# Sixteen fullest experts: stationary gate and up weights, tokens moving as one block

## The chip, the cores and the metric

The kernel runs on one core of a Trainium2 chip. The metric is the device time of one execution in microseconds (us). Five engines work side by side: TensorE (PE in the profile, with PEld for its weight loads), VectorE (DVE), ScalarE (ACT), GpSimd (POOL) and SyncE (SP), which here issues most DMA transfers. [...]

## The reference

One decoder layer on 2048 tokens of width 1024, in f32. After a mixer of a state space branch and a windowed attention branch comes the part that matters here, a hierarchical mixture of experts: each token picks one of 4 groups and in it the best 2 of 8 experts, so there are 4096 (token, expert) pairs over 32 experts. Then follow a gated embedding and a final norm. The expert is

```python
def expert_block(args):
    xb, e = args
    return (jax.nn.silu(xb @ w_eg[e]) * (xb @ w_eu[e])) @ w_ed[e]
```

with w_eg and w_eu of 1024 x 512 and w_ed of 512 x 1024. A token's two expert rows are weighted and added.

## The kernel before

**Precision.** Every large product is made of operands split in two parts, hi and lo, in a four-byte type for fast matmuls (fp32r). The product is hi*hi + hi*lo + lo*hi; the helper `mm3` (line 64) issues these three matmuls, which share nothing but their accumulator. A weight unit is 128 x 2048 (1 MB): SP fetches it to a raw buffer (`moe_raw`), ACT casts it to its hi part and DVE subtracts to get the lo part (`moe_split`, lines 1469 and 1470). There are four raw buffers and six pairs of hi and lo buffers, used in turn.

**Blocks of tokens.** The experts are ranked by their number of tokens (`route_tables`). Each rank has a slot of 128 rows; the 16 fullest have a second slot (slots 32 to 47): 128 rows for ranks 0 to 3 (`R1`), 64 rows for ranks 4 to 15 (`R2`). What exceeds these goes to `overflow`, a loop over blocks of 128 rows behind a branch on their number. `moe_in` gathers a slot's token rows from DRAM with an indirect DMA on POOL's queue and turns them on TensorE (line 1359: 8 transposes into PSUM, which ACT and DVE split into hi and lo).

**One expert.** `moe_gu` keeps the tokens stationary and moves the weights: for each of 8 slices k of the width, one matmul of 512 columns for each part of gate and of up. A slot of 128 rows takes 6 matmuls for each k. A slot of 64 rows is packed: its hi and lo tokens stand side by side as one stationary operand of 128 columns, 4 matmuls do for each k, and afterwards ACT copies one half of the result and DVE adds it to the other (lines 1390 to 1393). The result has the tokens on the partitions, so after silu and product `moe_act` turns it on TensorE (line 1409: 4 transposes for a slot) and splits it again. `moe_down` moves the two down units over it, 24 matmuls of 512 columns for 128 rows, 16 for a packed slot, evacuates the sums on ACT and DVE and scatters the rows with an indirect DMA.

**Order.** The experts run in pairs, a full one and an emptier one (ranks 0, 31, 1, 30, ...). In each step the next expert's tokens are fetched, then come this expert's gate and up, the expert before's down, and this one's activations:

```python
acts = self.moe_gu(xs, wt, nm)
if prev is not None:
    self.moe_down(*prev())
hl = self.moe_act(acts, nm)
```

The order inside each engine's queue is made from this program by a scheduler in the framework, which also sets the waits from the use of the buffers; each engine works its queue in order. Accumulators for gate, up and down share six PSUM banks (tag `acc`), the transposes two (tag `tp`). Turned tokens have three buffers for each part, activations three. After the experts, `proj_last` does the remaining part of an embedding projection, in the same buffers.

Of the kernel before, what the change touches and what calls it, by code (L numbers as in the profile page):

```python
# [11 lines left out]
F32 = mybir.dt.float32  # L12
# [11 lines left out]
NE = 32  # L24
NS1 = 48
R2 = 16
R1 = 4
NPA = 5
# [10 lines left out]
NUNIT = _n  # L39


class Kern:
# [1022 lines left out]
    def proj_last(self, n, m):  # L1065
# [137 lines left out]
    def route_tables(self, ctx):  # L1203
# [140 lines left out]
    def moe_in(self, idx, nm, rows=128):  # L1344
# [5 lines left out]
        xh = p.tile([128, 8, 128], F32R, tag="xh", name=f"xh{nm}", bufs=3)  # L1350
        if rows == 64:
            hi, lo = xh[:, :, 0:64], xh[:, :, 64:128]
        else:
            hi, lo = xh, p.tile([128, 8, 128], F32R, tag="xl", name=f"xl{nm}", bufs=3)
# [7 lines left out]
        return (xh, None) if rows == 64 else (hi, lo)  # L1362

    def moe_gu(self, xs, wt, nm):
# [3 lines left out]
        gu = [[ps.tile([128, 512], F32, tag="acc", name=f"{q}{n}", bufs=6) for q in "gu"] for n in nm]  # L1368
        for k in range(8):
            if k % 2 == 0:  # L1370
                wh, wl = wt[k // 2] if isinstance(wt, list) else wt(k // 2)
            s, e = k == 0, k == 7
            for (xh, xl), (g, u) in zip(xs, gu):
                cg = slice((k % 2) * 512, (k % 2) * 512 + 512)
                cu = slice(1024 + (k % 2) * 512, 1024 + (k % 2) * 512 + 512)
                pk = xl is None
                mm(g, xh[:, k], wh[:, cg], start=s, stop=False)  # L1377
                mm(g, xh[:, k], wl[:, cg], start=False, stop=pk and e)  # L1378
                mm(u, xh[:, k], wh[:, cu], start=s, stop=False)  # L1379
                mm(u, xh[:, k], wl[:, cu], start=False, stop=pk and e)  # L1380
                if not pk:
                    mm(g, xl[:, k], wh[:, cg], start=False, stop=e)  # L1382
                    mm(u, xl[:, k], wh[:, cu], start=False, stop=e)  # L1383
        res = []
        for n, (xh, xl), (g, u) in zip(nm, xs, gu):
            a = p.tile([128, 512], F32, tag="act", name=f"a{n}", bufs=3)
            if xl is None:
                a = a[0:64]
                b = p.tile([64, 2, 512], F32, tag="half", name=f"b{n}", bufs=1)
                nc.scalar.copy(b[:, 0], g[64:128])  # L1390
                nc.scalar.copy(b[:, 1], u[64:128])
                V.tensor_tensor(out=a, in0=g[0:64], in1=b[:, 0], op=ALU.add)
                V.tensor_tensor(out=b[:, 1], in0=u[0:64], in1=b[:, 1], op=ALU.add)
                nc.scalar.activation(a, a, AF.Silu)
                V.tensor_tensor(out=a, in0=a, in1=b[:, 1], op=ALU.mult)
            else:
                nc.scalar.activation(a, g, AF.Silu)
                V.tensor_tensor(out=a, in0=a, in1=u, op=ALU.mult)
            res.append(a)
        return res  # L1400

    def moe_act(self, acts, nm):
        nc, p, ps = self.nc, self.mp, self.mps
        hl = []
        for a, n in zip(acts, nm):
            rows = a.shape[0]
            tp = ps.tile([128, 4, 128], F32, tag="tp", name=f"ta{n}")[:, :, 0:rows]
            for k in range(4):
                nc.tensor.transpose(tp[:, k], a[:, k * 128:k * 128 + 128], self.ident[0:rows, 0:rows])  # L1409
            ah = p.tile([128, 4, 128], F32R, tag="ah", name=f"ah{n}", bufs=3)  # L1410
            if rows == 64:
                hi, lo = ah[:, :, 0:64], ah[:, :, 64:128]
            else:
                hi, lo = ah, p.tile([128, 4, 128], F32R, tag="al", name=f"al{n}", bufs=3)
            self.turned = [nc.scalar.copy(hi, tp).ins,  # L1415
                           nc.vector.tensor_tensor(out=lo, in0=tp, in1=hi, op=ALU.subtract).ins]
            hl.append((ah, None) if rows == 64 else (hi, lo))
        return hl

    def moe_down(self, hl, wt, dst, nm):  # L1420
# [3 lines left out]
        for j in range(2):  # L1424
            wh, wl = wt[j] if isinstance(wt, list) else wt(4 + j)
            js = slice(j * 512, j * 512 + 512)
            for (ah, al), yo, d, n in zip(hl, ys, dst, nm):
                y = ps.tile([128, 512], F32, tag="acc", name=f"y{n}{j}", bufs=6)
                rows = 64 if al is None else 128
                for k in range(4):  # L1430
                    c = slice(k * 512, k * 512 + 512)
                    if al is None:
                        mm(y, ah[:, k], wh[:, c], start=k == 0, stop=False)  # L1433
# [322 lines left out]
```

## Time and profile before

| | |
|---|---|
| timed runs | median 2347.01 us of 3 (2344.53 to 2348.16) |
| profiled execution | 2350.74 us, its span 2349.0 us |
| PE busy | 2261.8 us, 96%, 13948 matmuls |
| PEld busy | 1992.6 us |
| DVE busy | 1644.1 us, 70% |
| ACT busy | 1195.1 us, 51% |
| POOL busy | 364.1 us |
| DMA | 515.56 MB, mean 219 GB/s |

The expert stage runs from about 1300 to 2120 us of the span. The profile's matmul durations contain a pipeline's tail and overlap; what a matmul costs in a full queue is the distance from its start to the next start, which is read from the timeline. Records are labelled f32 in the rows for both four-byte types; a plain f32 matmul leaves two records, the fast type one.

### The profile page before, as it was taken

The numbers are of one execution on the slowest core, as the hardware profiler recorded it, in microseconds if no ns is written. First come the engines' busy times: TensorE is split into PE (matmuls) and PEld (weight loads), VectorE is DVE, ScalarE is ACT, GpSimd is POOL, SyncE is SP. The second block draws the span as 40 slices with busy tenths as digits, with TensorE's granted clock in tenths as the row PEclk, the third lists the DMA queues.
The fourth block names the chain that finished last, engine by engine and source line by source line (L and its number), as shares of the span: only waits on it lengthen the run. The fifth ranks groups of instructions, "written<-read, shape, count | busy, mean of one in ns | idle before, by whom it ended". The sixth has DMA issues, their size and how long they took to land. (4 is left out here: it accounts for less than half of the span.)

```text
span 2349.0 us, 36510 instructions
## 1 busy us (share of the span) xinstructions
PE 2261.8 (96%) x13948; PEld 1992.6 (85%) x13948; DVE 1644.1 (70%) x2666; ACT 1195.1 (51%) x1835; POOL 364.1 (16%) x282
## 2 busy tenths in 40 slices
PE   8889998899999999999999799999999999999997
PEld 8789996899999999998887588888887888877876
DVE  8777647788885334445667576677787777776998
ACT  7333335567664323222233565566666666664444
POOL 0043110221120000000001121121221112131122
PEclk9889999899999999999999799999999999999999
DMA  8385453643436546545444788888888888876552
GB/s 319 121 278 169 150 161 107 227 153 122 153 104 207 166 148 220 184 129 178 153 161 161 289 299 305 294 313 305 297 322 326 313 304 300 328 280 236 181 208 106
DMA packets 136082, 515.56 MB, mean 219 GB/s; under 512 B 16416, under 2 KB 34768, under 8 KB 108512
## 3 DMA queue, kind: packets, MB, share of 16 engines
q1 hardware_dynamic: 112544, 429.56, 53.2%
q0 software_dynamic: 23216, 83.37, 9.7%
q8 instruction: 111, 1.82, 0.3%
q14 instruction: 67, 0.55, 0.1%
q10 hardware_dynamic: 144, 0.26, 0.0%
HBM read 407.09 MB, written 102.77 MB: 217 GB/s over the span
## 5 line engine op out<-in xcount | busy, mean ns | idle before, releaser
L1470 DVE TENSOR_TENSOR e_l<-e_r,e_h 128x2048 fp32r<-128x2048 f32 x192 | 438.2, 2290 | 168.9 <-ACT e_h L1469 168.6
L1469 ACT CAST e_h<-e_r 128x2048 fp32r<-128x2048 f32 x192 | 366.3, 1911 | 156.8 <-PE us L1379 49.3
L1377 PE MATMUL gs<-e_h,xhs 128*128 128x512 f32 x384 | 153.1, 399 | 5.7 <-PEq L1530 5.7
L1379 PE MATMUL us<-e_h,xhs 128*128 128x512 f32 x384 | 153.6, 400 | 0.0
L1378 PE MATMUL gs<-e_l,xhs 128*128 128x512 f32 x384 | 150.6, 392 | 0.0
L1380 PE MATMUL us<-e_l,xhs 128*128 128x512 f32 x384 | 150.4, 392 | 0.0
L1445 POOL DMA_INDIRECT yb_d<-yos,rt x48 | 91.4, 1904 | 357.8 <-DVE yos L1441 129.6
L66 PE MATMUL ys<-e_h,ahs 128*128 128x512 f32 x288 | 114.2, 396 | 2.9 <-ACT ahs L1415 2.9
L67 PE MATMUL ys<-e_l,ahs 128*128 128x512 f32 x288 | 116.1, 403 | 0.0
L1348 POOL DMA_INDIRECT xgs<-h_d,rt x48 | 68.1, 1420 | 303.3 <-PE txs L1359 177.5
L68 PE MATMUL ys<-e_h,als 128*128 128x512 f32 x288 | 114.4, 398 | 0.0
L1383 PE MATMUL us<-e_h,xls 128*128 128x512 f32 x288 | 114.2, 397 | 0.0
L1382 PE MATMUL gs<-e_h,xls 128*128 128x512 f32 x288 | 113.3, 394 | 0.0
L68 PE MATMUL pz<-pg_h,pl 128*128 128x512 f32 (+1 forms) x264 | 103.2, 393 | 3.1 <-DVE pl L1591 2.8
L825 POOL TENSOR_TENSOR s<-s,dn 128x1024 f32<-128x1024 f32 (+1 forms) x32 | 63.2, 1975 | 276.9 <-DVE dn L824 159.9
L66 PE MATMUL pz<-pg_h,ph 128*128 128x512 f32 (+1 forms) x264 | 102.4, 389 | 0.0
L67 PE MATMUL pz<-pg_l,ph 128*128 128x512 f32 (+1 forms) x264 | 101.8, 386 | 0.0
L66 PE MATMUL u<-xh,u_h 128*128 128x256 f32 x256 | 72.4, 290 | 17.6 <-DVE ut L458 9.8
L1377 PEld LDWEIGHTS gs<-e_h,xhs 128*128 128x128 f32 x384 | 72.6, 189 | 19.5 <-issue 6.1
L1379 PEld LDWEIGHTS us<-e_h,xhs 128*128 128x128 f32 x384 | 72.4, 189 | 15.0
L1378 PEld LDWEIGHTS gs<-e_l,xhs 128*128 128x128 f32 x384 | 72.6, 189 | 14.5
L1380 PEld LDWEIGHTS us<-e_l,xhs 128*128 128x128 f32 x384 | 72.5, 189 | 14.1
(1484 smaller groups left out, 7337.2 us busy)
## 6 DMA issues: line engine op xcount, KB each, us to landing
e_r<-in_We SPq DMA_DIRECT2D x192, 1024.0 KB, 5.9
m_d<-mo SPq DMA_DIRECT2D x64, 256.0 KB, 3.4
yg<-yb_d SPq DMA_DIRECT2D x15, 1024.0 KB, 7.4
xt<-in_xT SPq DMA_DIRECT2D x16, 512.0 KB, 7.9
sq<-in_x SPq DMA_DIRECT2D x16, 512.0 KB, 5.3
m<-m_d SPq DMA_DIRECT2D x16, 512.0 KB, 5.2
xr<-in_x SPq DMA_DIRECT2D x16, 512.0 KB, 4.6
x_d<-xr POOLq DMA_DIRECT2D x16, 512.0 KB, 3.0
```

The costliest lines, as they stand in the source:

```text
L66: mm(out, ah, bh, start=start, stop=False)
L67: mm(out, ah, bl, start=False, stop=False)
L68: return mm(out, al, bh, start=False, stop=stop)
L1377: mm(g, xh[:, k], wh[:, cg], start=s, stop=False)
L1378: mm(g, xh[:, k], wl[:, cg], start=False, stop=pk and e)
L1379: mm(u, xh[:, k], wh[:, cu], start=s, stop=False)
L1380: mm(u, xh[:, k], wl[:, cu], start=False, stop=pk and e)
L1382: mm(g, xl[:, k], wh[:, cg], start=False, stop=e)
L1383: mm(u, xl[:, k], wh[:, cu], start=False, stop=e)
L1445: nc.gpsimd.indirect_dma_start(out=self.yb_d[:], out_offset=bass.IndirectOffsetOnAxis(ap=d[0:rows], axis=0), in_=yo[0:rows], in_offset=None)
L1469: nc.scalar.copy(hi, raw)
L1470: nc.vector.tensor_tensor(out=lo, in0=raw, in1=hi, op=ALU.subtract)
```

## The change

For the 16 experts with a second slot (`moe_gu_wide`) gate and up weights become the stationary operand, in pieces of 128 x 128, and both slots' tokens move as one block of n = 224, 192 or 160 rows (ranks 0 to 3, 4 to 7, 8 to 15): `more(r)` gives the second slot's 96, 64 or 32 rows. The hi and lo parts of the block lie side by side in one tile (`xw`), so one matmul with 2n columns does w_hi times both, and one with n columns does w_lo times hi. Hi and lo sums stand in two halves of a bank; ACT copies one half and DVE adds it to the other. The results have the hidden index on the partitions and go to `moe_down` without a transpose, after a cast and two subtracts. `moe_gu` for single slots now does 256 gate and 256 up columns at a time over all k, then the other half, since the weight units are cut anew: a unit holds 4 slices k of 256 gate and 256 up columns. Limits of the routing follow (`R3`, `cap`). Turned tokens have one buffer for each part, the block one, activations two.

```diff
 R2 = 16
+R3 = 8
 R1 = 4
+RM = 224
+def more(r):
+    return 32 * ((r < R1) + (r < R3) + (r < R2))
...
# proj_last
-            pr, hi, lo = f("xg", F32, "pr"), p.tile([128, 2, w], F32R, tag="xh", name=f"prh{g[0]}", bufs=3), \
-                p.tile([128, 2, w], F32R, tag="xl", name=f"prl{g[0]}", bufs=3)
+            pr, (t, b) = f("xg", F32, "pr"), ("x", 1) if w > 256 else ("a", 2)
+            hi, lo = (p.tile([128, 2, w], F32R, tag=t + q, name=f"pr{q}{g[0]}", bufs=b) for q in "hl")
...
# route_tables
         stt(cap, rank, R1 - 0.5, r2, ALU.is_lt, ALU.add)
+        stt(cap, rank, R3 - 0.5, cap, ALU.is_lt, ALU.add)
         ts(rk, rank, 128.0, None, ALU.mult)
-        ts(cap, cap, 64.0, 128.0, ALU.mult, ALU.add)
+        ts(cap, cap, 32.0, 128.0, ALU.mult, ALU.add)
...
+    def moe_gu(self, x, wt, nm):
+        nc, p, ps = self.nc, self.mp, self.mps
+        xh, xl = x
+        a = p.tile([128, 512], F32, tag="act", name=f"a{nm}", bufs=3)
+        for j in range(2):
+            gu = ps.tile([128, 512], F32, tag="acc", name=f"gu{nm}{j}", bufs=6)
+            for k in range(8):
+                if k % 4 == 0:
+                    wh, wl = wt[2 * j + k // 4] if isinstance(wt, list) else wt(2 * j + k // 4)
+                c = slice(k % 4 * 512, k % 4 * 512 + 512)
+                self.mm3(gu, xh[:, k], xl[:, k], wh[:, c], wl[:, c], k == 0, k == 7)
+            h = a[:, j * 256:j * 256 + 256]
+            nc.scalar.activation(h, gu[:, 0:256], AF.Silu)
+            nc.vector.tensor_tensor(out=h, in0=h, in1=gu[:, 256:512], op=ALU.mult)
+        return a
+
+    def moe_gu_wide(self, x, n, wt, nm):
+        nc, p, ps = self.nc, self.mp, self.mps
         V, mm = nc.vector, nc.tensor.matmul
+        m = n - 128
+        ahl = p.tile([128, 4, 2 * RM], F32R, tag="aw", name=f"aw{nm}", bufs=1)
+        for j in range(2):
+            acc = [ps.tile([128, 512], F32, tag="acc", name=f"w{nm}{j}{b}", bufs=6)[:, 0:2 * n] for b in range(4)]
+            for kh in range(2):
+                wh, wl = wt[2 * j + kh]
+                for b in (0, 2, 1, 3):
+                    for k in range(4):
+                        c = k * 512 + b * 128
+                        xk = x[:, 4 * kh + k]
+                        s, e = kh == k == 0, kh == 1 and k == 3
+                        mm(acc[b].rearrange("p (a n) -> p a n", a=2), wh[:, c:c + 128], xk, start=s, stop=False)
+                        mm(acc[b][:, 0:n], wl[:, c:c + 128], xk[:, 0], start=False, stop=e)
+            for b in range(2):
+                t = p.tile([128, 512], F32, tag="act", name=f"t{nm}{j}{b}", bufs=3)
+                g, u = t[:, 0:n], t[:, 256:256 + n]
+                aj = ahl[:, 2 * j + b]
+                for q, v in ((b, g), (2 + b, u)):
+                    nc.scalar.copy(v, acc[q][:, n:2 * n])
+                    V.tensor_tensor(out=v, in0=acc[q][:, 0:n], in1=v, op=ALU.add)
+                nc.scalar.activation(g, g, AF.Silu)
+                V.tensor_tensor(out=g, in0=g, in1=u, op=ALU.mult)
+                nc.scalar.copy(aj[:, 0:n], g)
+                V.tensor_tensor(out=aj[:, n + m:2 * n], in0=g[:, 0:128], in1=aj[:, 0:128], op=ALU.subtract)
+                V.tensor_tensor(out=aj[:, n:n + m], in0=g[:, 128:n], in1=aj[:, 128:n], op=ALU.subtract)
+        return [(ahl[:, :, 0:128], ahl[:, :, n + m:2 * n], 128),
+                (ahl[:, :, 128:n + m], None, m) if m <= 64 else (ahl[:, :, 128:n], ahl[:, :, n:n + m], m)]
...
# moe, fetch
+            x = self.mp.tile([128, 8, 2, RM], F32R, tag="xw", name=f"xw{slots[0]}", bufs=1)[:, :, :, 0:128 + m]
+            for q, (s, w) in enumerate(zip(slots, (128, m))):
+                self.moe_in(ix[q], f"s{s}", w, x, 128 * q)
...
# moe, the loop
+            wide = rows > 128
+            acts = self.moe_gu_wide(x, rows, wt, nm[0]) if wide else self.moe_gu(x, wt, nm[0])
             if prev is not None:
                 self.moe_down(*prev())
-            hl = self.moe_act(acts, nm)
+            hl = acts if wide else self.moe_act(acts, nm[0])
...
# pack, on the host: the new weight units
-        return w.reshape(NE, 4, 2, 128, 512).transpose(0, 1, 3, 2, 4)
-    gu = np.stack([rows(g["w_e_gate"][0]), rows(g["w_e_up"][0])], 3).reshape(NE, 4, 128, 2048)
+        return w.reshape(NE, 2, 4, 128, 2, 256).transpose(0, 4, 1, 3, 2, 5)
+    gu = np.stack([rows(g["w_e_gate"][0]), rows(g["w_e_up"][0])], 5).reshape(NE, 4, 128, 2048)
```

`moe_down` takes each block's rows with it: blocks of 64 rows and fewer are packed as before, others (now also 96 rows) take three matmuls for each k.

## Rows read from the trace of the kernel before

**Rows 1.** the page, busy time of an engine, share of the span, instructions.
```profile
PE 2261.8 (96%) x13948; PEld 1992.6 (85%) x13948; DVE 1644.1 (70%) x2666; ACT 1195.1 (51%) x1835; POOL 364.1 (16%) x282
```

**Rows 2.** who waits for whom, PE, 1250 to 2130 us (total us, times, longest).
```profile
PE txs L1359 <- DMA xgs<-h_d,rt: 7.6, 1, 7.6
PE gs L1377 <- PEq L1530: 5.7, 1, 5.7
PE txs L1359 <- DVE xls L1361: 3.0, 1, 3.0
PE ys L66 <- ACT ahs L1415: 2.9, 1, 2.9
```

**Rows 3.** windows: length, then busy us of each engine, PE's granted clock, DMA share, GB/s.
```profile
1500.00:1600.00 100.00, 100.00 (x472) 81.33 (x471) 75.26 (x58) 63.89 (x61) 19.74 (x12) 1.00 0.84 310
1800.00:1900.00 100.00, 100.00 (x471) 80.37 (x470) 77.96 (x63) 65.89 (x62) 17.54 (x13) 1.00 0.87 311
```

**Rows 4.** timeline, gate and up: start us, duration us, engine, line, operation.
```profile
1399.82 0.39 PE L1378 MATMUL gs<-e_l,xhs 128*128 128x512 f32 x1
1401.41 0.39 PE L1379 MATMUL us<-e_h,xhs 128*128 128x512 f32 x1
```

**Rows 5.** timeline, down.
```profile
1411.47 0.40 PE L66 MATMUL ys<-e_h,ahs 128*128 128x512 f32 x1
1414.28 0.40 PE L66 MATMUL ys<-e_h,ahs 128*128 128x512 f32 x1
```

**Rows 6.** timeline, matmuls of 256 columns in the gates' stage.
```profile
899.82 0.28 PE L67 MATMUL gz<-gh1070l,gB_h 128*128 128x256 f32 x1
903.94 0.28 PE L66 MATMUL gz<-gh1071h,gB_h 128*128 128x256 f32 x1
```

**Rows 7.** timeline, transposes (eight merged in one row).
```profile
1406.17 1.04 PE L1359 MATMUL txs<-ident,xgs 128*128 128x128 f32 x8
1522.04 0.71 PE L1359 MATMUL txs<-ident,xgs 64*128 64x64 f32 x8
```

**Rows 8.** groups by line and form, PE, 1300 to 2130 us (busy us, mean ns).
```profile
L1377 PE MATMUL gs<-e_h,xhs 128*128 128x512 f32 x384 | 153.1, 399 | 5.7 <-PEq L1530 5.7
L1409 PE MATMUL tas<-ident,as 128*128 128x128 f32 x144 | 21.1, 272 | 0.0
L1409 PE MATMUL tas<-ident,as 64*128 64x64 f32 x48 | 5.5, 235 | 0.0
```

**Rows 9.** the same of PEld, the whole span.
```profile
L967 PEld LDWEIGHTS lg<-h2l,wrhl 128*36 128x36 f32 x56 | 6.2, 112 | 1.0 <-DVE h2l L961 0.7
L968 PEld LDWEIGHTS lg<-h2h,wrhl 128*72 128x72 f32 x64 | 9.1, 142 | 1.5 <-ACT h2h L960 0.6
L1377 PEld LDWEIGHTS gs<-e_h,xhs 128*128 128x128 f32 x384 | 72.6, 189 | 19.5 <-issue 6.1
L1359 PEld LDWEIGHTS txs<-ident,xgs 64*128 64x128 f32 x96 | 7.6, 138 | 8.4 <-DVE xhs L1361 4.0 <-issue 3.7 <-DVE xls L1361 0.7
```

**Rows 10.** timeline, plain f32 of 128 columns (two records in a row).
```profile
339.98 0.39 PE L568 MATMUL op<-uT,t 128*128 128x128 f32 x2
341.10 0.39 PE L571 MATMUL op<-S,ca 128*128 128x128 f32 x2
```

**Rows 11.** groups by line and form, DVE and ACT, 1300 to 2130 us.
```profile
L1470 DVE TENSOR_TENSOR e_l<-e_r,e_h 128x2048 fp32r<-128x2048 f32 x191 | 436.0, 2290 | 168.9 <-ACT e_h L1469 168.6
L1361 DVE TENSOR_TENSOR xls<-txs,xhs 128x512 fp32r<-128x512 f32 x72 | 48.6, 684 | 13.6 <-ACT xhs L1360 9.2 <-DMA pp_d<-po 4.3
L1361 DVE TENSOR_TENSOR xhs<-txs,xhs 128x256 fp32r<-128x256 f32 x24 | 9.8, 412 | 0.0
L1469 ACT CAST e_h<-e_r 128x2048 fp32r<-128x2048 f32 x190 | 362.7, 1911 | 156.8 <-PE us L1379 49.3 <-PE us L1383 42.3 <-PE ys L1433 36.2
L1360 ACT CAST xhs<-txs 128x512 fp32r<-128x512 f32 x72 | 41.5, 585 | 30.4 <-PE txs L1359 30.4
L1360 ACT CAST xhs<-txs 128x256 fp32r<-128x256 f32 x24 | 8.8, 371 | 0.3
```

More of the change, by code (lines that the diff above doesn't have):

```diff
@@ L1341, in row_index, with moe_in @@
         return done
-    def moe_in(self, idx, nm, rows=128):
+    def moe_in(self, idx, nm, rows=128, into=None, at=0):
         nc, p, ps = self.nc, self.mp, self.mps
@@ L1349, in moe_in @@
                                      in_offset=bass.IndirectOffsetOnAxis(ap=idx[0:rows], axis=0))
-        xh = p.tile([128, 8, 128], F32R, tag="xh", name=f"xh{nm}", bufs=3)
-        if rows == 64:
-            hi, lo = xh[:, :, 0:64], xh[:, :, 64:128]
+        if into is None:
+            hi, lo = (p.tile([128, 8, 128], F32R, tag=f"x{q}", name=f"x{q}{nm}", bufs=1) for q in "hl")
         else:
-            hi, lo = xh, p.tile([128, 8, 128], F32R, tag="xl", name=f"xl{nm}", bufs=3)
+            hi, lo = into[:, :, 0, at:at + rows], into[:, :, 1, at:at + rows]
         for h in range(2):
@@ L1366, in moe_gu @@
+    def moe_gu_wide(self, x, n, wt, nm):
         nc, p, ps = self.nc, self.mp, self.mps
         V, mm = nc.vector, nc.tensor.matmul
[L1368 to L1399, printed above, removed]
@@ L1400, in moe_gu @@
-        return res
-    def moe_act(self, acts, nm):
-        nc, p, ps = self.nc, self.mp, self.mps
[L1404 to L1418, printed above, removed]
+        m = n - 128
@@ new lines, in moe_gu_wide, with moe_act @@
+        return [(ahl[:, :, 0:128], ahl[:, :, n + m:2 * n], 128),
+                (ahl[:, :, 128:n + m], None, m) if m <= 64 else (ahl[:, :, 128:n], ahl[:, :, n:n + m], m)]
+    def moe_act(self, a, nm):
+        nc, p, ps = self.nc, self.mp, self.mps
+        tp = ps.tile([128, 4, 128], F32, tag="tp", name=f"ta{nm}")
+        for k in range(4):
+            nc.tensor.transpose(tp[:, k], a[:, k * 128:k * 128 + 128], self.ident)
+        hi, lo = (p.tile([128, 4, 128], F32R, tag=f"a{q}", name=f"a{q}{nm}", bufs=2) for q in "hl")
+        self.turned = [nc.scalar.copy(hi, tp).ins,
+                       nc.vector.tensor_tensor(out=lo, in0=tp, in1=hi, op=ALU.subtract).ins]
+        return [(hi, lo, 128)]
@@ L1426, in moe_down @@
             js = slice(j * 512, j * 512 + 512)
-            for (ah, al), yo, d, n in zip(hl, ys, dst, nm):
+            for (ah, al, rows), yo, d, n in zip(hl, ys, dst, nm):
                 y = ps.tile([128, 512], F32, tag="acc", name=f"y{n}{j}", bufs=6)
-                rows = 64 if al is None else 128
                 for k in range(4):
@@ L1432, in moe_down @@
                     if al is None:
[L1433 to L1434 removed]
+                        mm(y[0:2 * rows], ah[:, k], wh[:, c], start=k == 0, stop=False)
+                        mm(y[0:2 * rows], ah[:, k], wl[:, c], start=False, stop=k == 3)
                     else:
[L1436 removed]
+                        last = self.mm3(y[0:rows], ah[:, k], al[:, k], wh[:, c], wl[:, c], k == 0, k == 3)
                 if al is None:
[L1438 to L1439 removed]
+                    nc.scalar.copy(yo[0:rows, js], y[rows:2 * rows])
+                    nc.vector.tensor_tensor(out=yo[0:rows, js], in0=y[0:rows], in1=yo[0:rows, js], op=ALU.add)
                 elif j:
[L1441 removed]
+                    self.downed = nc.vector.tensor_copy(yo[0:rows, js], y[0:rows]).ins
                 else:
[L1443 removed]
+                    nc.scalar.copy(yo[0:rows, js], y[0:rows])
                 if j:
@@ L1492, in fetch @@
         def fetch(slots):
-            return [self.moe_in(self.IDX[:, s:s + 1], f"s{s}", 64 if s >= 32 + R1 else 128) for s in slots]
+            ix = [self.IDX[:, s:s + 1] for s in slots]
+            if len(slots) == 1:
+                return self.moe_in(ix[0], f"s{slots[0]}"), 128
+            m = more(slots[0])
+            x = self.mp.tile([128, 8, 2, RM], F32R, tag="xw", name=f"xw{slots[0]}", bufs=1)[:, :, :, 0:128 + m]
+            for q, (s, w) in enumerate(zip(slots, (128, m))):
+                self.moe_in(ix[q], f"s{s}", w, x, 128 * q)
+            return x, 128 + m
         self.wslots((), range(3))
```

13 lines of the change are left out of this document (3 added, 10 removed).

## The prediction

> **What bounds the kernel now.** I read the page first: the matrix engine (PE) is busy for 96% of the span [rows 1]. Then the waits of PE over the whole expert stage: 7.6 us for the first gathered tokens, 5.7 us at the overflow branch, 3.0 us at the second turn, 2.9 us before the last down projection, one of each, and nothing else of weight [rows 2]. Between these PE waits for nothing, and the windows say the same: from 1500 us on PE is busy throughout at a granted clock of 1.00, with VectorE (DVE) at 75 to 78%, ACT at 64 to 66% and the DMA engines at 84 to 87% [rows 3]. So the expert stage is a sum of PE's starts; every nanosecond taken from a matmul's spacing comes off the end, as long as nobody else becomes late. Ends of matmuls overlap, so I count from start to start.
>
> The spacings are: a gate/up matmul with 512 moving columns, seven starts in 1.59 us, 0.227 us each [rows 4]; a down matmul, twelve in 2.81 us, 0.234 us [rows 5]; a matmul with 256 moving columns, 35 in 4.12 us, 0.118 us [rows 6]. Eight transposes of 128 columns last 1.04 us with a tail of about 0.27, so 0.110 us each; of 64 columns, (0.71 - 0.235) / 7 = 0.068 us ([rows 7], the tails from [rows 8]).
>
> **Gate and up of the sixteen wide experts.** L1377 ran 384 times, 8 for each of 48 slots [rows 8]; a slot of 128 rows takes 6 matmuls for each of 8 k (20 such slots are in wide experts), each of the 12 packed ones 4. So an expert with two full slots costs 96 x 0.227 = 21.8 us (4 of them), one with a packed second slot 80 x 0.227 = 18.2 us (12). Afterwards each expert has 64 pairs (2 x 2 x 4 x 4): one matmul with 2n moving columns, one with n, for n = 224 (4 experts), 192 (4), 160 (8). The wide one lies between the measured 256 and 512 columns; on their line (0.109 us over 256 columns) it takes 0.145, 0.173, 0.200 us for n = 160, 192, 224.
>
> The narrow one has no row: no matmul in this operand type moves under 256 columns. Its bounds:
> - Below, the same line carried on: 0.077, 0.091, 0.104 us. That needs weights that load faster than that.
> - In the middle, the weight load. The loads' durations grow evenly: 36 columns 112 ns, 72 columns 142 ns, 128 columns 189 ns [rows 9], so 0.83 ns a column, and 128 columns occupy 107 ns behind a fixed latency of about 82 ns. (A transpose's load lasts only 138 ns, 56 ns over the same latency, and those do come every 68 ns.) A matmul whose own columns need less than 107 ns would then come every 0.118 us, as at 256 columns, where load and columns are equally long.
> - Above, the plain f32 matmul: 128 columns are two records of 0.112 us each (ten starts in 1.12 us) [rows 10], so 0.28, 0.34, 0.39 us.
>
> I take the middle, 0.118 us, since it rests on the loads of just this type. An expert then costs 64 x (0.145 + 0.118) = 16.9 us, 18.6 us, 20.3 us, and the sixteen change by 8 x (16.9 - 18.2) + 4 x (18.6 - 18.2) + 4 x (20.3 - 21.8), unrounded **-14.6 us**. Below it would be -46 us, above +194 us. The moving columns fall by 18%, but half of the new matmuls don't get their share of it: with 192 rows the expert even gets slower.
>
> [...]
>
> **Transposes.** A wide expert's activations come out with the hidden index on the partitions, so its 4 transposes per slot go: of the 144 of 128 columns and the 48 of 64 [rows 8], 80 and all 48, 80 x 0.110 + 48 x 0.068 = **-12.1 us**. Gathered tokens are still turned; 32 turns of 128 columns become 96 columns (by the line between 0.068 and 0.110, -0.02 us each), 64 of 64 become 32 (between 0 and half, I take none): **-0.7 us** (to -2.9).
>
> **Down.** The second block of 96 rows keeps three matmuls for each k, those of 64 and 32 rows the packed two; all still move 512 columns and their number stays 1056: 0. The narrow experts keep 48 gate/up matmuls, now half after half; if these take the down spacing, 768 x 0.007 = +5 us; I take 0, as the pattern of operands is the old one.
>
> **ACT and DVE.** From 512 to 256 columns a subtract falls from 684 to 412 ns and a cast from 585 to 371 ns [rows 11], so about 140 ns + 1.06 ns a column, and 157 + 0.84. Each wide expert gets four groups of 4 ACT operations of n columns and of 3 DVE operations of n and two of 128 and n - 128. For n = 160 that is 4.7 us of ACT and 5.5 us of DVE; for 224, 5.5 and 6.6. Gone are, with a full second slot, 2.4 and 2.7 us; with a packed one some 3.4 and 3.8 us. Over the sixteen about +30 us of ACT and, after some -3 us on the turned tokens, +35 us of DVE. In a stage of some 770 us (1350 to 2120), shortened a little, DVE goes from 78% to about 85%, ACT from 65% to about 71%. PE hides both as long as none of their results is late.
>
> What can be late is an accumulator. Six banks serve gate/up and down; a wide half takes four, so the second half's third and fourth must take over the first half's first two. By the order 0, 2, 1, 3 the first bank is complete 24 matmuls (3.1 us) before its half ends and is wanted 8 matmuls (1.0 us) into the next: 4.2 us for a copy of 0.29 and an add of 0.31 us. But they queue in order behind the weight units' casts of 1.91 us and subtracts of 2.29 us [rows 11]. One of each is 4.2 + 0.6 = 4.8 us: now and then just late. Bounds: 0, and two of each at every expert, (9.0 - 4.2) x 16 = 77 us; I take **+4 us**, near the first, since ACT spends 157 us of the stage waiting, mostly for PE to release weight slots [rows 11], and the weights are thus not in a hurry.
>
> Single buffers for turned tokens and activations: their last reader is in each case one expert back, 9 us or more of PE work before; 0, at most some 3 us in all as with the 3.0 us of [rows 2]. The same for the projection at the end, whose parts take these buffers. The added DVE operation in the routing tables has 32 columns, by the line above under 0.2 us. Transfers: the weights' bytes stay, the gathered and scattered rows fall by 7%; a stage 3% shorter puts the engines at some 88%, and with four raw buffers nobody waits for them. The reference's inputs send 210, 208, 198, 176 tokens to the four fullest experts, 165 to 155 to the next four, 154 to 130 to the next eight and 125 at most to the others, so no block overflows with the new sizes.
>
> **Sum.** -14.6 - 12.1 - 0.7 + 4 + 0.2 = -23 us. The profiled execution took 2350.7 us (span 2349.0); less 23, 2327.5. The three timed runs have their median 3.7 us under it, so I forecast 2324 us; its own range, with stalls of 0 to 15 us and the small bounds, is 2311 to 2337.
>
> **Rivals.**
> 1. Weight loads hidden (below): -46 in place of -14.6, so -54 in all, 2293. For it: a load's duration is latency too, and its occupancy is only inferred. Against: the slope over three widths that ends at just the 107 ns. [...]
> 2. The narrow matmul at the plain f32 rate (above): +194 - 12.1 - 0.7 + 4, 2532 us, slower. It decides from 0.118 + 0.023 = 0.141 us a matmul (23 us over 1024). For it: the operands have four bytes, and nothing in the trace shows this type below 256 columns. Against: one record for each matmul here, two for plain f32; an array that streams columns has no cause to slow for fewer of them.
> 3. Late accumulators take the bound: 27 us of PE time are given back when each of the 16 experts loses 1.7 us in the middle; with all waits of two casts and subtracts, +50 us, 2397. For it: DVE at 85% and strict order. Against: PE never waited for an accumulator before, though with two or four of the six banks at a time.
>
> **Chances.** Forecast 0.56, rival 1 0.13, rival 2 0.11, rival 3 0.20, half of it ending within 0.2% (4.7 us, about what can be told from no change) and half above. Faster 0.56 + 0.13 = 0.69, same 0.10, slower 0.21. The range reaches from rival 1 with a few us to spare, 2285, to the middle of rival 3's slow half, 2372; left out are rival 2 and a few hundredths.
>
> **What would show it.** Starts of wl matmuls (n columns) 0.118 us before the next one whatever n is, and the pairs 0.26, 0.29 and 0.32 us apart: the weight load bounds. Pairs of 0.22 us at n = 160: rival 1. Pairs above 0.4 us or two records each: rival 2. PE waits for DVE adds at the third and fourth bank of a second half, with DVE over 85%: rival 3. No activation transposes but for the narrow experts' 64. The forecast is wrong if a pair of n = 160 is under 0.24 us or over 0.30 us.

## The result and the profile after

| | before | after |
|---|---|---|
| timed runs, median us | 2347.07 (2344.53 to 2348.16, 4 runs) | 2311.47 (2309.99 to 2313.57, 4 runs) |
| ratio, 95% interval | 1 | 0.9859 [0.9844, 0.9875] |
| profiled execution, its span | 2350.74, 2349.0 | 2310.56, 2308.8 |

On another chip the same two kernels had 2345.04 us (seven runs; an eighth, in a slow state, took 4475.18) and 2311.4 us, ratio 0.986 [0.9842, 0.9878]. The change takes 35.6 us off; 23 were forecast. The two profiled executions lie 40.2 us apart. Here is where these are, from start to start of PE's matmuls:

| stretch | before | after | difference |
|---|---|---|---|
| start of the span to the routing table's first sum | 1274.9 | 1270.4 | -4.5 |
| from there to the first gate/up matmul | 41.9 | 52.3 | +10.4 |
| first gate/up to last down | 804.0 | 760.9 | -43.1 |
| from there to the end | 228.2 | 225.2 | -3.0 |

The first row I count as no effect of the change: in the profiled executions of this study the first gates' matmul, long before the change's place, starts anywhere from 421.7 to 429 us, and the kernel before is at the late end with 429.2 (426.3 after). The third row is the forecast's subject, and it holds almost twice the forecast -23.4; the second was not foreseen. Within the third:

| PE, start to next start, us | before | after | difference | forecast |
|---|---|---|---|---|
| gate/up, 16 wide experts | 313.5 | 289.1 | -24.4 | -14.6 |
| gate/up, 16 narrow experts | 180.0 | 183.8 | +3.8 | 0 |
| activations' transposes, with the wait before the last down | 21.1 | 8.0 | -13.1 | -12.1 |
| tokens' transposes | 33.8 | 32.5 | -1.2 | -0.7 |
| down | 252.9 | 246.6 | -6.3 | 0 |
| accumulator stalls | 0 | 0 | 0 | +4 |
| projection's matmuls within the stage | 2.7 | 0.9 | -1.8 (done later) | |

The page after, its first line (busy us, share of the span, instructions), answers to [rows 1]; PE stays at 96%, with 576 matmuls more and 46 us less:

```profile
PE 2215.5 (96%) x14524; PEld 1997.4 (87%) x14524; DVE 1659.7 (72%) x2915; ACT 1209.8 (52%) x2019; POOL 364.7 (16%) x282
```

The windows of [rows 3], after (length; busy us of PE, PEld, DVE, ACT, POOL; granted clock; DMA share; GB/s):

```profile
1500.00:1600.00 100.00, 100.00 (x559) 87.27 (x558) 79.39 (x96) 67.41 (x85) 23.02 (x14) 1.00 0.87 316
1800.00:1900.00 100.00, 100.00 (x594) 86.04 (x593) 81.55 (x96) 69.97 (x88) 22.82 (x13) 1.00 0.92 336
```

PE is still busy throughout at a clock of 1.00, DVE went from 75-78% to 79-82% (85 forecast), ACT to 67-70 (71 forecast), the DMA engines to 87-92 (88 forecast): nobody else became the bound. PE's waits from 1250 to 2130 us (total, times, longest) answer to [rows 2]:

```profile
PE txs L1366 <- DMA xgs<-h_d,rt: 22.8, 1, 22.8
PE ws L1405 <- PEq L1550: 3.6, 1, 3.6
PE pt L1609 <- DVE x L1598: 1.1, 2, 0.9
...
PE ys L73 <- ACT ahs L1428: 0.8, 1, 0.8
```

No accumulator is in the list, and the 2.9 us ahead of the last down fell to 0.8; in the table above this wait stands with the transposes, the operation in front of it, so the transposes alone fell by 11. But the first gathered tokens now cost PE 22.8 us in place of 7.6. POOL's own waits from 1250 to 1350 us, the gather's line, tell why. After:

```profile
POOL xgs L1356 <- PE txs L1366: 34.1, 3, 11.8
POOL xgs L1356 <- DMA pp_d<-po: 22.3, 1, 22.3
```

and before:

```profile
POOL xgs L1348 <- PE txs L1359: 24.5, 2, 15.8
...
POOL xgs L1348 <- DVE rt L1339: 10.8, 1, 10.8
```

Before, the first gather was released by the routing table that it reads. After, it waited for something that it does not read at all: the transfer that stores `po`, tiles of an earlier stage. That is a buffer's address: `xw` is now allocated ahead of the gather buffers `xg` and pushed them from bytes 149344-157536 of each partition to 163680-171872, where the earlier pool had `po` (162656-174944). The gather may not write until those are stored.

The pairs, n = 160, as the timeline shows them after (start us, duration us, engine, line, operation; PEld are loads of the stationary operand):

```profile
1813.06 0.23 PE L1406 MATMUL ws<-xw,e_l 128*128 128x160 f32 x1
1813.06 0.19 PEld L1405 LDWEIGHTS ws<-xw,e_h 128*128 128x128 f32 x1
...
1813.13 0.34 PE L1405 MATMUL ws<-xw,e_h 128*128 128x320 f32 x1
1813.17 0.19 PEld L1406 LDWEIGHTS ws<-xw,e_l 128*128 128x128 f32 x1
1813.32 0.23 PE L1406 MATMUL ws<-xw,e_l 128*128 128x160 f32 x1
1813.32 0.19 PEld L1405 LDWEIGHTS ws<-xw,e_h 128*128 128x128 f32 x1
1813.39 0.35 PE L1405 MATMUL ws<-xw,e_h 128*128 128x320 f32 x1
...
1813.43 0.19 PEld L1406 LDWEIGHTS ws<-xw,e_l 128*128 128x128 f32 x1
...
1813.57 0.24 PE L1406 MATMUL ws<-xw,e_l 128*128 128x160 f32 x1
```

A pair takes 0.26 us (1813.06, .32, .57). Medians over the stage are 0.257, 0.285 and 0.314 us for n = 160, 192, 224 (forecast 0.263, 0.291, 0.318). The w_hi load starts together with the w_lo matmul, and the w_lo load 0.108 us behind it (median over the stage), while the w_hi matmul is under way. So w_hi's load has only the short w_lo matmul (160 columns, by estimate 0.067 us) to lie beside, and w_lo's has the long one. The estimate, here and below, counts 2.4 columns a ns: the kernel before starts its first gate/up matmuls, of 512 columns, 0.427 us apart at a granted clock of 0.50 (median of eleven distances, 1317.42 to 1322.11 us), 1.2 columns a ns, and I take twice that at 1.00. The records divide the pair differently than I wrote: w_lo to w_hi 0.073 us, w_hi to w_lo 0.184. So what w_hi waits for its weights seems to stand in its own distance; the next experiment bears that out.

### The profile page after: what moved, and what is told of

The parts are those of the page before. It is cut to its first block, busy times and chain, and to the rows that moved or that the text cites. A ratio compares the mean times of both kernels' runs of the same rounds, so it can differ in the third digit from the quotient of the medians.

```text
span 2308.8 us, 38073 instructions
## 1 busy us (share of the span) xinstructions
PE 2215.5 (96%) x14524; PEld 1997.4 (87%) x14524; DVE 1659.7 (72%) x2915; ACT 1209.8 (52%) x2019; POOL 364.7 (16%) x282
## 5 line engine op out<-in xcount | busy, mean ns | idle before, releaser
L1405 PE MATMUL ws<-xw,e_h 128*128 128x320 f32 (+2 forms) x1024 | 290.5, 359 | 3.6 <-PEq L1550 3.6
L1406 PE MATMUL ws<-xw,e_l 128*128 128x160 f32 (+2 forms) x1024 | 251.8, 248 | 0.0
L1405 PEld LDWEIGHTS ws<-xw,e_h 128*128 128x128 f32 x1024 | 192.2, 189 | 7.6 <-issue 3.9
L1406 PEld LDWEIGHTS ws<-xw,e_l 128*128 128x128 f32 x1024 | 195.9, 192 | 0.0
L73 PE MATMUL gus<-e_h,xhs 128*128 128x512 f32 x256 | 102.9, 402 | 0.0
L75 PE MATMUL gus<-e_h,xls 128*128 128x512 f32 x256 | 102.7, 401 | 0.0
L74 PE MATMUL gus<-e_l,xhs 128*128 128x512 f32 x256 | 101.6, 397 | 0.0
L73 PE MATMUL u<-xh,u_h 128*128 128x256 f32 x256 | 72.8, 291 | 18.5 <-DVE ut L465 9.8
L829 ACT ACTIVATE s<-s,m 128x256 f32<-128x256 f32 (+1 forms) x128 | 62.7, 492 | 36.5 <-DVE m L823 34.4
L74 PE MATMUL u<-xl,u_h 128*128 128x256 f32 x256 | 73.6, 291 | 0.0
L75 PE MATMUL u<-xh,u_l 128*128 128x256 f32 x256 | 72.8, 287 | 0.0
L1366 PE MATMUL txs<-ident,xgs 128*128 128x128 f32 (+3 forms) x384 | 48.8, 264 | 23.4 <-DMA xgs<-h_d,rt 22.8
```

What stands on the lines that cost most here:

```text
L73: mm(out, ah, bh, start=start, stop=False)
L74: mm(out, ah, bl, start=False, stop=False)
L75: return mm(out, al, bh, start=False, stop=stop)
L829: A.activation(s[:, i], s[:, i], AF.Exp, bias=m[:, i:i + 1], accum_out=dn[:, i:i + 1])
L1366: nc.tensor.transpose(tp[:, k], xg[0:rows, kk * 128:kk * 128 + 128], self.ident[0:rows, 0:rows])
L1405: mm(acc[b].rearrange("p (a n) -> p a n", a=2), wh[:, c:c + 128], xk, start=s, stop=False)
```

## Experiments

### Which load, which columns

Three kernels change one operand of the pair each. In the first, w_lo's matmuls move 64 columns whatever n is (the products of the other tokens with w_lo are left out):

```diff
-                        mm(acc[b][:, 0:n], wl[:, c:c + 128], xk[:, 0], start=False, stop=e)
+                        mm(acc[b][:, 0:64], wl[:, c:c + 128], xk[:, 0, 0:64], start=False, stop=e)
```

> The changed kernel, but the w_lo matmul of a wide expert moves only 64 of its n token columns (w_lo times x_hi is left out for the other rows). Pairs (from one w_hi matmul to the next) are now 0.257, 0.285, 0.313 us for n = 160, 192, 224. Theory A (the 107 ns load of the next w_hi runs only beside the short w_lo matmul and is what is waited for; a pair is 0.108 + 2n/2.4 + 0.015 us): the pairs stay, 2311 us, 2305 to 2316. Theory B (moving columns bound): 0.040, 0.053, 0.067 us less for each pair, -51 us, 2260.

Measured 2311.8 us, wide experts' gate/up 291.5 us (289.1 without the edit; the difference is the first expert's, which here ran longer at a granted clock of 0.50, the 15 others agree within 0.1 us each). The timeline:

```profile
1812.53 0.19 PE L1406 MATMUL ws<-xw,e_l 128*128 128x64 f32 x1
1812.53 0.19 PEld L1405 LDWEIGHTS ws<-xw,e_h 128*128 128x128 f32 x1
1812.56 0.39 PE L1405 MATMUL ws<-xw,e_h 128*128 128x320 f32 x1
...
1812.79 0.19 PE L1406 MATMUL ws<-xw,e_l 128*128 128x64 f32 x1
```

96 columns fewer, and the pair is still 0.26 us: the w_hi matmul starts 0.03 after w_lo instead of 0.07, and lasts 0.23 to the next start instead of 0.18. What the columns give, the load takes. This shows w_lo's columns to be free here.

The second and third load 64 weight columns in place of 128 in seven of eight w_hi (w_lo) loads; half the hidden units lose these products:

```diff
-                        mm(acc[b].rearrange("p (a n) -> p a n", a=2), wh[:, c:c + 128], xk, start=s, stop=False)
+                        h = 128 if s else 64
+                        mm(acc[b].rearrange("p (a n) -> p a n", a=2)[0:h], wh[:, c:c + h], xk, start=s, stop=False)
```

> The changed kernel, but 7 of 8 w_hi matmuls load and use only 64 of their 128 weight columns (half of w_hi's product is left out); columns moved as before. Theory A (w_hi's load is the exposed one): it falls to 54 ns and hides beside the w_lo matmul of 67 to 93 ns; pairs of about 0.220, 0.260, 0.300 us, -25 us, 2286. Theory C (the load of w_lo is the late one, as its matmul starts 184 ns after a w_hi matmul that needs 133): no change, 2311. Theory B: no change, 2311.

```diff
-                        mm(acc[b][:, 0:n], wl[:, c:c + 128], xk[:, 0], start=False, stop=e)
+                        h = 128 if e else 64
+                        mm(acc[b][0:h, 0:n], wl[:, c:c + h], xk[:, 0], start=False, stop=e)
```

> The changed kernel, but 7 of 8 w_lo matmuls load and use only 64 of their 128 weight columns (half of w_lo's product is left out). Theory A: w_lo's load is hidden beside the long w_hi matmul anyway, no change, 2311, pairs 0.257, 0.285, 0.313. Theory C: the pair falls by up to 0.04 us, -25 to -40 us, 2271 to 2286.

With w_hi's loads halved (timeline, same columns):

```profile
1802.43 0.23 PE L1407 MATMUL ws<-xw,e_l 128*128 128x160 f32 x1
1802.43 0.13 PEld L1406 LDWEIGHTS ws<-xw,e_h 128*64 128x64 f32 x1
1802.51 0.30 PE L1406 MATMUL ws<-xw,e_h 128*64 128x320 f32 x1
1802.51 0.19 PEld L1407 LDWEIGHTS ws<-xw,e_l 128*128 128x128 f32 x1
...
1802.65 0.23 PE L1407 MATMUL ws<-xw,e_l 128*128 128x160 f32 x1
```

The pair is 0.22 us and the wide experts' gate/up 264.7 us, -24.4 as the theory of the exposed w_hi load gave. With w_lo's loads halved:

```profile
1812.47 0.24 PE L1407 MATMUL ws<-xw,e_l 128*64 128x160 f32 x1
1812.48 0.19 PEld L1405 LDWEIGHTS ws<-xw,e_h 128*128 128x128 f32 x1
1812.55 0.34 PE L1405 MATMUL ws<-xw,e_h 128*128 128x320 f32 x1
1812.59 0.14 PEld L1407 LDWEIGHTS ws<-xw,e_l 128*64 128x64 f32 x1
1812.73 0.24 PE L1407 MATMUL ws<-xw,e_l 128*64 128x160 f32 x1
```

0.26 us again, 289.5 us in all, 2313.25 us: no gain. So of the two loads only w_hi's is on the path. All three fit one rule: a pair takes the larger of two sums, w_hi's load and its own 2n columns (0.108 us + 2n columns at 2.4 a ns + 0.015 us: 0.256, 0.283, 0.310 us), or all 3n columns (3n at 2.4 a ns + 0.018 us: 0.218, 0.258, 0.298; the pairs of the kernel with halved w_hi loads are 0.22, 0.26, 0.30). The 0.108 is the distance of the two loads' starts above; 0.015 and 0.018 are fitted. The rule holds within 4 ns for the widths that it was fitted to; pairs of n = 256 in a kernel below take 0.350 us, 12 ns more than it gives, and why is open. What the load costs is thus, by the estimate of 2.4 columns a ns, 0.108 us less n columns, 41 ns at n = 160 and 15 at 224.

That kernel, though, took 2297.8 us, only some 13.5 less than the changed kernel: 11 of the 24 us came back. Its PE waits, 1250 to 2130 us:

```profile
PE pp L75 <- POOL prl L1084: 6.6, 1, 6.6
PE pt L1610 <- DVE x L1599: 4.1, 2, 3.7
```

These two are at the end of the stage: when PE gets through the experts sooner, POOL's and DVE's work on the projection's parts is late. The changed kernel has no row of the first, and 1.1 us of the second. So of these 24 us only some 13 reach the end while that work stays as it is.

A fourth kernel groups four w_hi matmuls, then four w_lo. It should say whether the alternation matters. By my mistake it was built on the kernel of the section on addresses below, not on the changed one as its expectation says, so it is to be read against that one's 2295.0 us and 288.9 us of wide gate/up:

```diff
+                    for k in range(4):
+                        c = k * 512 + b * 128
+                        mm(acc[b].rearrange("p (a n) -> p a n", a=2), wh[:, c:c + 128], x[:, 4 * kh + k],
+                           start=kh == k == 0, stop=False)
+                    for k in range(4):
+                        c = k * 512 + b * 128
+                        mm(acc[b][:, 0:n], wl[:, c:c + 128], x[:, 4 * kh + k, 0], start=False, stop=kh == 1 and k == 3)
```

> The changed kernel with the same matmuls in another order: of each group of four slices k first the four w_hi matmuls, then the four w_lo ones. Theory A: of the four w_lo matmuls each again has a load of 107 ns beside it (three of w_lo, one of w_hi), so a group of four costs the same 4 x 0.257 us or, with one more fixed cost for each, up to 4 x 0.263: 2311 to 2317. Theory C (only the change from w_hi to w_lo is slow): three of four such changes go, -0.04 us each, about -30 us, 2281.

Measured 2294.67 us, 289.0 us of wide gate/up: the order alone does nothing. By the reading above it could not: in groups, too, four of eight loads lie beside a short w_lo matmul (three of w_lo and one of w_hi).

### What the finer blocks bring

Weights stationary, but blocks of 256 and 192 rows as before the change:

```diff
-RM = 224
+RM = 256
 def more(r):
-    return 32 * ((r < R1) + (r < R3) + (r < R2))
+    return 64 * ((r < R1) + (r < R2))
...
-        stt(cap, rank, R3 - 0.5, cap, ALU.is_lt, ALU.add)
-        ts(cap, cap, 32.0, 128.0, ALU.mult, ALU.add)
+        ts(cap, cap, 64.0, 128.0, ALU.mult, ALU.add)
```

> The changed kernel with the block sizes of before: 256 rows for ranks 0 to 3, 192 for ranks 4 to 15; gate and up weights still stand. Theory A: pairs of 0.108 + 0.213 + 0.015 = 0.336 us and 0.285 us in place of 0.313 (4 experts) and 0.257 (8): 4 x 64 x 0.023 + 8 x 64 x 0.028 = +20 us, 2331; so standing weights alone gain only the transposes and what lies around. Theory B (each column removed counts 1/2.4 ns, three columns for each row): 4 x 64 x 0.040 + 8 x 64 x 0.040 = +31 us, 2342.

Measured 2336.28 us (2335.36 to 2337.41), ratio to before 0.9965 [0.9952, 0.9979]; wide gate/up 313.2 us. That lies between the figures expected: at 192 rows the pairs are 0.285 us as theory A had them, at 256 rows 0.350 in place of 0.336. The stationary weights by themselves leave gate and up where they were (313.5). For each k, 256 rows move 8 x 3 x 256 = 6144 columns, as many as the 12 matmuls of 512 before; 192 rows move 4608 against 5120, and w_hi's loads take that back (18.4 us an expert against 18.5). What the standing weights gain within the stage is the 13 us of transposes with the wait beside them and 5 us of down (252.9 to 247.6), less 4 us that the narrow experts lose; part of it is lost again at the start of the stage. The 24 us of gate/up come from the finer blocks: 224 rows move 5376 columns for each k, 160 rows 3840, a quarter under the 5120 of a full and a packed slot.

### Addresses

Only the order in which buffers get their addresses is changed: gather, output and activation tiles are named before `xw`, so the gather buffers lie at 149344-157536 again; no instruction is added to any engine:

```diff
+        for t, w, n, dt in (("xg", 1024, 2, F32), ("yo", 1024, 2, F32), ("ah", 512, 2, F32R), ("al", 512, 2, F32R), ("aw", 8 * RM, 1, F32R)):
+            for q in range(n):
+                self.mp.tile([128, w], dt, tag=t, name=f"at_{t}{q}", bufs=n)
```

> The changed kernel with other addresses alone: the gathered tokens' two buffers stand first in their pool, as before the change, and the block xw last, so that no gather writes where the projection's outputs still wait for their stores. Theory D (the first gather of the expert stage waited 11 to 12 us for these stores, seen as a wait of POOL for the pp_d transfers until 1305 us): -10 us, 2301, the first gather about 1 us after its indices. Rival: the stage was waiting for weights or the branch anyway, no change, 2311.

Measured 2295.0 us (2293.02 to 2295.84), ratio to before 0.9786 [0.9768, 0.9803], 16.4 us under the changed kernel where 10 were expected. PE's waits, 1250 to 2130 us, and then POOL's, 1250 to 1350 us, of this kernel:

```profile
PE txs L1366 <- DMA xgs<-h_d,rt: 7.4, 1, 7.4
PE ws L1405 <- PEq L1554: 6.4, 1, 6.4
```

```profile
POOL xgs L1356 <- PE txs L1366: 36.2, 4, 11.1
...
POOL xgs L1356 <- DVE rt L1347: 10.8, 1, 10.8
```

The wait for `po` is gone, the gather waits for its table once more, and the first gate/up matmul starts at 1310.2 us in place of 1322.7: 12.5 us, the cause of the late start, shown. (From the routing table's first sum to that matmul, the second row of the first table, the six kernels with the gather buffers first took 39.7 to 41.1 us, the seven runs with them behind `xw` 51.0 to 52.3, the kernel before 41.9.) The rest came from where I expected nothing: down fell from 246.6 to 241.7 us. The same matmuls of the changed kernel:

```profile
1777.06 0.39 PE L73 MATMUL ys<-e_h,ahs 128*128 128x512 f32 x1
...
1781.27 0.39 PE L73 MATMUL ys<-e_h,ahs 128*128 128x512 f32 x1
```

and of this one:

```profile
1761.40 0.39 PE L73 MATMUL ys<-e_h,ahs 128*128 128x512 f32 x1
...
1763.44 0.39 PE L73 MATMUL ys<-e_h,ahs 128*128 128x512 f32 x1
```

18 starts in 4.21 us (0.234 each) against 9 in 2.04 (0.227). The activations' tiles had moved from 186304-194496 to 165728-173920, those of the wide experts from 202688-209856 to 173920-181088. So the 0.227 and 0.234 us of [rows 4, 5], which the prediction took as properties of two kinds of matmul, seem to hang on where the tiles of the stationary operand lie. To test that, the narrow experts' tokens, whose gate/up matmuls come every 0.234 us in this kernel and the changed one, were put low as well:

```diff
-... ("xg", 1024, 2, F32), ("yo", 1024, 2, F32), ("ah", 512, 2, F32R), ...
+... ("xg", 1024, 2, F32), ("xh", 1024, 1, F32R), ("xl", 1024, 1, F32R), ("ah", 512, 2, F32R), ...
```

> As the kernel with the gather buffers allocated first (2295.0 us), but the narrow experts' turned tokens (one tile for hi, one for lo) are allocated right behind the gather buffers, at 157536 to 165728 bytes of a partition, where before the change the tokens' tiles began, in place of 201664 to 209856; only addresses differ. Theory A (a matmul's spacing hangs on where its stationary tile lies): the narrow experts' gate and up matmuls come every 227 ns in place of 234, 768 of them, -5.4 us: 2290. Theory B (the half after half order sets the 234): spacing unchanged, 2295. As the weights are prefetched less far when PE is faster, a part of the 5 us may be given back at the stage's end.

Measured 2290.44 us (2288.83 to 2292.29; on a third chip, where the kernel before took 2345.6), ratio 0.9764 [0.9748, 0.9781]. The narrow experts' gate/up matmuls, median spacing 227 ns:

```profile
1812.36 0.39 PE L73 MATMUL gus<-e_h,xhs 128*128 128x512 f32 x1
...
1813.72 0.39 PE L73 MATMUL gus<-e_h,xhs 128*128 128x512 f32 x1
```

Six starts in 1.36 us; in the changed kernel:

```profile
1700.10 0.40 PE L73 MATMUL gus<-e_h,xhs 128*128 128x512 f32 x1
...
1701.51 0.39 PE L73 MATMUL gus<-e_h,xhs 128*128 128x512 f32 x1
```

six in 1.41. Their sum fell by 5.1 us (183.7 to 178.6), the run by 4.6: the address theory holds, and the half after half order does not set the 0.234. With the hi part low and the lo part high (`xl` left out of the list, 157536 and 197568):

> As the kernel with low addresses for both parts of the narrow experts' tokens, but only the hi part is low (157536), the lo part lies at 197568; the activations' tiles lie at 161632 to 176992. Of the three matmuls for each k the first two have the hi part as the stationary operand, the third the lo part. Theory A1 (the address of the tile whose load is exposed sets its own matmul's spacing): two starts 227 ns apart, one 234, in every three. A2 (any load from a high address): the same, but shifted by one. Theory B (order or pattern, not addresses): all 234.

Measured 2292.79 us, one run, and spacing medians of 233, 232 and 232 ns for the three matmuls of a k: neither two fast and one slow nor all 234. A high lo tile slows all three, a little less than two high tiles. That the addresses decide is shown; by what rule is open.

### Accumulators

Five banks in place of six:

```diff
-            acc = [ps.tile([128, 512], F32, tag="acc", name=f"w{nm}{j}{b}", bufs=6)[:, 0:2 * n] for b in range(4)]
+            acc = [ps.tile([128, 512], F32, tag="acc", name=f"w{nm}{j}{b}", bufs=5)[:, 0:2 * n] for b in range(4)]
```

(and so for the three other users of the banks)

> The changed kernel with five accumulator banks for gate, up and down in place of six; nothing else. With six banks PE never waited for an accumulator, although the prediction gave +4 us for it. Theory A (the slack was larger than predicted): a half's first bank is complete 24 matmuls before the half ends, and with six banks it is wanted by the next half's third bank, which begins 16 matmuls into it, not 8 as the prediction counted: 40 matmuls or 20 pairs, 5.1 us at 160 rows. With five it is wanted by the second bank, 32 matmuls or 16 pairs, 4.1 us later, just what the prediction had put as the slack, against its 4.8 us of delay in the worst usual case: 0.7 us now and then, 0 to 16 us in all, 2312 to 2325, with waits of PE for DVE's adds or ACT's copies by name. Theory B (adds and copies are never near late, as ACT and DVE have their queues short): no such wait, 2311. Theory C (they queue behind two casts and two subtracts, 9 us): over 40 us of waits, above 2350.

Measured 2317.88 us, one run, its span 2316.1 against 2308.8. No wait of PE names an accumulator, and no distance between two starts in the stage is over 0.42 us but the two that the changed kernel has too. The stage took 763.6 us in place of 760.9; the other 4.6 us lie before and behind it, where executions differ by as much. So the copies and adds are not late even with the shorter slack: theory B by the waits. The 2.7 us have no row that names them. The edit also changed the order that the scheduler made: the gathered tokens' transposes break into gate/up at 51 places where it was 32, and 77 of the gate/up starts are over 0.25 us where 57 were, most of them beside transposes. That these account for the 2.7 us is likely, but not shown.

### A faster version

Since a load beside a short w_lo matmul is exposed (by the estimate above for 41 ns at n = 160), w_lo's loads can be made shorter, so that in groups only one load of w_hi in four is still in the way: w_lo in bf16 (the same tile, half its bytes unused), with a bf16 copy of x_hi made by POOL, four w_hi matmuls and then four w_lo; with the addresses of the kernel above. One of the three products is thus coarser.

```diff
+                nc.gpsimd.tensor_copy(xb[:, 4 * h:4 * h + 4, at:at + rows], hi[:, 4 * h:4 * h + 4])
...
+        if half:
+            lo = lo.bitcast(BF16)[:, 0:2048]
...
+                        mm(acc[b][:, 0:n], wl[:, c:c + 128], xb[:, 4 * kh + k], start=False, stop=kh == 1 and k == 3)
```

> As the one with other addresses, and the low part of the gate and up weights of wide experts, with a copy of the high part of the tokens, in bf16, the four w_hi matmuls of a group before its four w_lo ones; the projection at the end keeps three tiles in place of four. Bf16 loads with 128 x 96 products came every 46 ns in the routing tables. Theory A: w_lo's loads then hide beside each other, only one load of w_hi in four is exposed: per pair about 0.230, 0.267, 0.305 us, -20 us against the one with other addresses, 2281. If the order or the type brings nothing: 2301.

Measured 2284.18 us (2281.19 to 2287.18), ratio 0.9744 [0.9725, 0.9764]; wide gate/up 266.2 us, -22.7, of which 10.8 reached the end. The order alone had brought nothing (above), so the type is needed; the type without the order was not run. The loads of this kernel, 1300 to 2130 us (busy us, mean ns):

```profile
L1406 PEld LDWEIGHTS ws<-xw,e_h 128*128 128x128 f32 x1024 | 163.0, 191 | 9.2 <-issue 7.1
L1410 PEld LDWEIGHTS <-e_l 128*128 128x128 bf16 x1024 | 71.0, 98 | 34.9 <-issue 22.3
```

A bf16 load's record lasts 98 ns, one of the four-byte type 191. (The routing tables' bf16 loads that the expectation names start 42 ns apart in the traces of the kernels before and after, not 46.) With the narrow tokens' tiles low in addition:

> The kernel with bf16 w_lo and a bf16 copy of x_hi for w_lo's matmuls (2284.2 us) with the same addresses for the narrow experts' tokens as in the kernel beside it. Theory A (addresses): another -5 us, 2279, unless the waits at the stage's end, where 11 us were given back before, take it: then 2284 with PE's waits for the projection's transposes and for DVE grown by as much. Theory B: 2284 with spacings unchanged.

Measured 2277.34 us (2272.2 to 2278.39), ratio 0.9706 [0.9686, 0.9726], the best of the study. Its timeline (four instructions merged in a row):

```profile
1777.86 0.45 PE L1410 MATMUL ws<-xb,e_l 128*128 128x160 bf16 x4
1778.11 0.82 PE L1406 MATMUL ws<-xw,e_h 128*128 128x320 f32 x4
1778.77 0.45 PE L1410 MATMUL ws<-xb,e_l 128*128 128x160 bf16 x4
```

Four pairs take 0.91 us, 0.228 each. The window from 1800 us, columns as above:

```profile
1800.00:1900.00 100.00, 100.00 (x602) 82.57 (x601) 88.63 (x105) 72.10 (x92) 36.68 (x27) 1.00 0.96 348
```

Its PE waits, 1250 to 2130 us:

```profile
PE pt L1620 <- DVE x L1609: 5.7, 1, 5.7
PE pp L73 <- DVE yos L1454: 1.4, 1, 1.4
```

With DVE at 89% and the DMA engines at 96%, a part of the gain comes back in waits for DVE.

## Why the prediction came out as it did

**The mechanism held.** The forecast took for the narrow matmul the larger of its columns and the weight load, 0.118 us, and the pairs came out 4 to 6 ns under it. Matmuls of 512 columns stayed at 0.227 to 0.234 us. Rival 1 (loads hidden, a pair of 0.22 us) is what the kernel with halved w_hi loads shows, so it was a true alternative and the load is what excludes it. Rival 2 (plain f32 rate) is dead: each matmul below 256 columns is one record, and between 160 and 224 columns its distance grows by 28 ns, 0.44 ns a column. One sign that I named was wrong: I looked for the wait at w_lo's own start ("0.118 us before the next one whatever n is"); it shows in w_hi's distance, and w_lo's varies with n, 73, 85, 101 ns.

**Gate and up, -14.6, measured -20.6.** The term's error lies in the kernel before, not in the new one. After, the sixteen cost 289.1 us against 290.6 by the forecast's pairs: the even pairs are 6 us less than that, and late starts, at half the clock or beside other operations, give 4 back. Before, I multiplied 0.227 us by 1344 matmuls, 305 us; they took 313.5, a mean of 0.233, since 0.227 is what a good stretch shows [rows 4]. The 8 us between have three parts. The first 13 starts, 2.7 us too long, fell into a stretch at half the clock (granted 0.50 from 1298.6 to 1322.5 us; PE was busy for 3.9 of the 18.2 us ahead of these starts):

```profile
1317.42 0.63 PE L1378 MATMUL gs<-e_l,xhs 128*128 128x512 f32 x1
1317.84 0.63 PE L1379 MATMUL us<-e_h,xhs 128*128 128x512 f32 x1
```

44 more were over 0.25 us, each the start after the first matmul behind a transpose, 3.9 us in all, and the rest had a mean of 0.228, 1.6 us. (The changed kernel starts its gate/up at half the clock too, with 2 us in its first expert.) Against this the narrow experts lost 3.8 us. The prediction had named that price ("if these take the down spacing, 5 us") and chosen 0 because the operands' pattern was the old one; the pattern was not what mattered, the tiles' addresses were.

**Transposes -12.1 and -0.7, measured -13.1 and -1.2.** Right within about a microsecond each; of the 13.1, 2.1 are the shorter wait ahead of the last down, which was no part of the term, and 11 the transposes.

**Down 0, measured -6.3.** The count stayed at 1056 and the mean went from 0.2395 to 0.2335 us. The addresses are hardly in it: the activations lie elsewhere than before (188352 to 200640 then), but the median start is 0.234 us apart in both kernels. What fell is the number of starts over 0.25 us, 63 before and 13 after; they stood beside transposes, of which fewer are left and fewer break into down. They make 5.5 of the 6.3 us. The prediction counted the matmuls and took each at the even spacing, before and after.

**Accumulators +4, measured 0.** I wrote that the first half's first bank is wanted 8 matmuls into the next half. It is the third bank in the order that takes it over, 16 matmuls in, so the slack was 40 matmuls or 5.1 us at n = 160, not 4.2. That removes the reason for the term; that there is no wait with five banks either says that the queueing of two long operations in front of a copy was assumed too readily. Rival 3 held 0.20 of the chance on that assumption.

**The start of the stage, not in the sum: +10.4.** "Single buffers ... 0" looked at who reads a buffer last within the stage. It did not ask where the new buffers lie and what lay there before. The 14 KB of `xw` moved the gather buffers onto tiles still being stored, and the first gather, on the path that starts the stage, waited 22 us. The kernel with the gather buffers first shows it: 12.5 us.

So the forecast was right in sign, in mechanism and in range; the median is 12.5 us under it, at the edge of the range that the sum gave (2311 to 2337). That it is inside that range is luck: without the 10.4 us lost at the start, which no term held, it would have been 2301. Of the 20 us that the stage gained beyond the forecast, 6.0 are gate/up (mostly the size of the old cost), 6.3 down, 4 the stall that did not come, 1.5 transposes, and 1.8 work moved behind the stage; 10.4 were lost at its start.

## What to carry to other kernels

When matmuls of unequal length alternate, look at which load lies beside the short one: here its exposed part was the load's 0.108 us less the columns of the matmul beside it, 41 ns at n = 160 by the estimate, and only the columns of the other were still worth saving (96 fewer beside the load left the pair at 0.26 us). For an old cost take the sum over all starts and not the spacing of a good stretch. A new buffer in a pool moves the others: before building, list what each first writer of a buffer will find at its new address, above all at the start of a stage.

## What was not expected of the hardware

The spacing of back-to-back 512-column matmuls of 128 x 128 weights was 227 ns with the stationary tiles at bytes 157536 to 182112 of a partition, and 233 to 234 with them at 178112 to 186304, 186304 to 200640 or 201664 to 209856, in programs that differ in the addresses alone for the two moves tested: 3% of PE's time in these stages, 10 us over down and the narrow experts' gate/up. With one of two tiles high it was 232 to 233. The lowest of the slow ranges overlaps the fast one by 4 KB, and there the same place does both: before the change a lo tile at 178016 to 182112 had 227 ns beside hi tiles further down, after it a hi tile at 178112 to 182208 had 234 beside a lo tile above. So a tile's own address does not decide alone; the other tile of the product counts too, as in the kernel with one tile high. No experiment tells the height of the addresses from what else is read at the time, so this stays an observation.

For the loads, the timeline of the changed kernel shows how far ahead they run: in the rows shown w_hi's load starts with the w_lo matmul in front of its own (both at 1813.06 and at 1813.32 us) and not earlier, so here a load had one matmul to hide behind.
